# Cumulative log decays as rows through DRAM, in place of 32 products on TensorE

## The chip, the cores and the metric

The program runs on one core of a Trainium2 chip. The metric is device time in microseconds (us), taken as the median of several executions; beside them one execution was recorded by the hardware profiler.

## What is computed

The program runs two blocks on a sequence of 256 tokens of width 1024, all in fp32. The change lies in the hybrid mixer of the first block, and there in its Mamba-2 part (SSD), which has 16 heads in 2 groups of 8 and chunks of 128 tokens. Cut to what matters:

```python
a = (dt * A).reshape(b, nc, chunk, G, E)            # log decays
acs = jnp.cumsum(a, axis=2)                         # their sums along a chunk
seg = acs[:, :, :, None] - acs[:, :, None, :]       # (t, s) differences, per head
Lm = jnp.exp(jnp.where(mask, seg, -jnp.inf))        # causal decays
CB = jnp.einsum('bctgn,bcsgn->bctsg', C, B)
y_diag = jnp.einsum('bctsg,bctsge,bcsgep->bctgep', CB, Lm, xd)
```

For each of 2 chunks and 16 heads a 128x128 matrix of differences `seg` is needed: the sum at token t, which varies along the free dimension of a tile, less the sum at token s, which is the partition.

## The kernel before

Tokens come as two tiles of 128. Every large product is made as three products of fp32r halves (`mm3`, lines 277 to 279): each operand is split into a high part on ScalarE (`split`, line 203) and a low part on VectorE (line 207). Weights arrive by DMA in units of 1 MB into a ring of 3 buffers (`raw`, issued on the SyncE queue at line 258), and are split in halves into rings of 4 buffers (`hi`, `lo`). So a weight's load waits until the unit three earlier has been split, and a split waits until the products on the half four earlier are done. All these waits stand in the engines' own queues, which run strictly in order.

The hybrid mixer weaves two generators. `products` makes projections that need little beside TensorE; `chain` makes the SSD and then the mLSTM, and says at its yields how many steps of `products` go in between. The stages of `chain` that matter here:

- the log decays `a` (line 622) and, by products with the triangular mask `tri`, their sums by column, `cs` (lines 624 to 627);
- B and C: two weight groups, each followed by a causal convolution (`conv`, lines 635 to 642: one copy on ScalarE, then three dependent steps on VectorE) and a Silu into `bc`;
- `inputs(g)`: the same convolution for the x of one head group. Four accumulators `t2` come out of it, each turned by two TensorE transposes (line 663) that stand in TensorE's queue between the products;
- `states(g)`: the Silu of x, the factors of dt, and the chunk's state;
- `decays(g)`: for each chunk and head, line 687 multiplies the head's column of `a`, broadcast to 128 columns, with `tri`. This gives the sums as a row, the same on every partition; line 690 subtracts the column `cs` on VectorE and caps it, line 695 takes the exponential on ScalarE, and line 696 multiplies by the products of C and B;
- `outputs(g)`: the products with `seg`, gating and a norm.

Outside stretches that are marked `manual_schedule`, the order on each engine is not that of the code: a scheduler, which works with estimates of how long everything takes, sets it at build time. The hybrid part lies outside such stretches until its last projection.

Of the kernel before, what the change touches and what calls it, by code (L numbers as in the profile page):

```python
# [12 lines left out]
AF = mybir.ActivationFunctionType  # L13
# [91 lines left out]
class Net:  # L105
# [43 lines left out]
    def dram(self, shape):  # L149
        self.n += 1  # L150
        return self.dp.tile(shape, F32, name=f"dram{self.n}")

    def load_const(self, name, cols, parts=128):
        t = self.const(cols, parts=parts)
        self.nc.sync.dma_start(t, self.ins[name])
        return t
# [405 lines left out]
class Hybrid:  # L562
    def hybrid(self, then):
        nc = self.nc
        ins = self.ins
        V, A, PE, G = nc.vector, nc.scalar, nc.tensor, nc.gpsimd
        mm = PE.matmul
# [4 lines left out]
        def products():  # L572
# [24 lines left out]
            for g in range(2):  # L597
# [3 lines left out]
                    A.activation(so[t, g], p, AF.Sigmoid)  # L601
                yield

        def chain():

            fill = iter(FILL)
# [13 lines left out]
            V.memset(coef[:, 16:], -1.0)  # L620
            a = self.small(40).rearrange("p (t c) -> p t c", t=2)
            V.tensor_tensor(a, sp, coef[:, None, :].to_broadcast([128, 2, 20]), OP.mult)
            pc = self.pt()
            mm(pc[:, :40], self.tri, a.rearrange("p t c -> p (t c)"), start=True, stop=True)
            mm(pc[:, 64:80], self.after, a[:, 0, :16], start=True, stop=True)
            cs = self.small(40).rearrange("p (t c) -> p t c", t=2)
            V.tensor_copy(cs.rearrange("p t c -> p (t c)"), pc[:, :40])
            ecs, de = self.small(16), self.small(16)
            A.activation(ecs, cs[:, 1, :16], AF.Exp)
            A.activation(de, pc[:, 64:80], AF.Exp)  # L630
            dt = sp

            cw = self.col("hy_cw").rearrange("p (j k) -> p j k", k=5)
# [15 lines left out]
                    acc = conv(j, ps[i][:, :256])  # L649
                    A.activation(bc[:, j], acc.rearrange("p (t c) -> p t c", t=2), AF.Silu)  # L650

            xs, xd, st, px, seg, yv = {}, {}, {}, {}, {}, {}
            e8 = lambda z: z.rearrange("p (e q) -> p e q", e=8)

            def inputs(g):
# [23 lines left out]
            def decays(g):  # L679

                for c in range(2):
                    seg[c] = self.g().rearrange("p (e t) -> p e t", e=8)
                    for hb in range(2):
                        pr = self.pt().rearrange("p (e t) -> p e t", e=4)
                        for e in range(4):
                            h = g * 8 + hb * 4 + e
                            mm(pr[:, e, :], a[:, c, h:h + 1].to_broadcast([128, 128]), self.tri, start=True, stop=True)  # L687
                        for e in range(4):
                            h = g * 8 + hb * 4 + e
                            V.scalar_tensor_tensor(seg[c][:, hb * 4 + e, :], pr[:, e, :], cs[:, c, h:h + 1], self.cap,  # L690
                                                   op0=OP.subtract, op1=OP.min)
                for c in range(2):
                    for hb in range(2):
                        half = seg[c][:, hb * 4:hb * 4 + 4]
                        A.activation(half, half, AF.Exp)
                        V.tensor_tensor(half, half, cb[:, c, g, None, :].to_broadcast([128, 4, 128]), OP.mult)

            def outputs(g):
                for c in range(2):
                    py = e8(self.pt())  # L700
                    for e in range(8):
                        mm(py[:, e, :], seg[c][:, e, :], xd[c, g][:, e, :], start=True, stop=True)
                    dx = e8(self.t2())
                    G.tensor_tensor(dx, xs[c, g], self.row("hy_d")[:, g * 8:g * 8 + 8, None].to_broadcast([128, 8, 64]), OP.mult)
                    V.tensor_tensor(dx, py, dx, OP.add)
                    if c:
                        po = self.pt()
                        mm(po, bc[:, 2 + g, 1, :], st[g], start=True, stop=True)
                        yo = e8(self.t2())
                        V.tensor_tensor(yo, e8(po), ecs[:, g * 8:g * 8 + 8, None].to_broadcast([128, 8, 64]), OP.mult)  # L710
                        V.tensor_tensor(dx, dx, yo, OP.add)
                    y = yv[c] = dx.rearrange("p e q -> p (e q)")
                    V.tensor_tensor(y, y, zs[c][:, g * 512:(g + 1) * 512], OP.mult)
                    ss = self.small(1)
                    A.activation(self.junk[:, :512], y, AF.Square, accum_out=ss)
                    r = self.rsqrt(ss, 1, 1.0 / 512)
                    V.tensor_scalar(y, y, r, None, op0=OP.mult)

            def turn(g):
                for c in range(2):  # L720
                    self.flip(yv[c], cat_y, g, c, self.col("hy_sn")[:, 4 * g:4 * g + 4])
# [17 lines left out]
            yield next(fill)  # L739
            inputs(1)  # L740
            outputs(0)
            yield next(fill)
            turn(0)
            states(1)
# [37 lines left out]
            for hb in range(2):  # L782
                pr = self.pt().rearrange("p (h c s) -> p h c s", h=2, c=2)
# [22 lines left out]
            for h in range(4):  # L806
                p = self.pt()
# [4 lines left out]
            for c in range(2):  # L812
                for h in range(4):
                    p = self.pt()
# [10 lines left out]
            for c in range(2):  # L825
# [8 lines left out]
                r = self.rsqrt(ss, 4, 1.0 / 256)  # L834
# [975 lines left out]
```

## Time and profile before

| | |
|---|---|
| median of 3 executions | 1719.06 us (1717.37 to 1719.6) |
| the profiled execution | 1717.73 us |
| its span, first to last instruction | 1715.9 us |
| TensorE (PE) busy | 1686.2 us, 98% of the span |
| VectorE (DVE) busy | 1130.9 us, 66% |
| ScalarE (ACT) busy | 896.4 us, 52% |
| GpSimd (POOL) busy | 299.4 us, 17% |
| share of TensorE in the chain of work that ended last | 82% |
| mean granted TensorE clock | 0.992 of full speed |

The hybrid part takes about 204 to 360 us of the span, and the stages above lie between 215 and 300 us. In the profile's rows a TensorE instruction's end is modelled, so two rows that follow each other overlap; the time that one takes of the engine is the distance from its start to the next start. The same is true, less strongly, of the other engines. An fp32 product appears as two records.

### The profile page before, as it was taken

The numbers are of one execution on the slowest core, as the hardware profiler recorded it, in microseconds if no ns is written. First come the engines' busy times: TensorE is split into PE (matmuls) and PEld (weight loads), VectorE is DVE, ScalarE is ACT, GpSimd is POOL, SyncE is SP. The second block draws the span as 40 slices with busy tenths as digits, with TensorE's granted clock in tenths as the row PEclk, the third lists the DMA queues.
The fourth block names the chain that finished last, engine by engine and source line by source line (L and its number), as shares of the span: only waits on it lengthen the run. The fifth ranks groups of instructions, "written<-read, shape, count | busy, mean of one in ns | idle before, by whom it ended". The sixth has DMA issues, their size and how long they took to land.

```text
span 1715.9 us, 27060 instructions
## 1 busy us (share of the span) xinstructions
PE 1686.2 (98%) x10518; PEld 1495.0 (87%) x10518; DVE 1130.9 (66%) x2203; ACT 896.4 (52%) x1329; POOL 299.4 (17%) x458
## 2 busy tenths in 40 slices
PE   9999999999999999999899999999999999999998
PEld 8998799788999899988689998888898878889886
DVE  7665588656665566647956664657775765778566
ACT  7443476464444354434465444567446446644643
POOL 3000021002000010000331000234532113364211
PEclk9999999999999999999899999999999999999999
DMA  7555453444555555554125556445443544554442
GB/s 274 197 176 205 150 193 127 147 152 159 194 193 188 176 193 191 182 205 161 68 99 180 189 189 212 167 153 168 142 151 143 184 165 175 149 163 158 146 148 96
DMA packets 63440, 287.65 MB, mean 168 GB/s; under 512 B 23760, under 2 KB 26704, under 8 KB 30288
## 3 DMA queue, kind: packets, MB, share of 16 engines
q1 hardware_dynamic: 63312, 285.92, 48.3%
q8 instruction: 83, 1.36, 0.3%
q14 instruction: 45, 0.37, 0.1%
HBM read 283.28 MB, written 2.62 MB: 167 GB/s over the span
## 4 chain that ended last, share of the span: by engine, by line
PE 82%; DVE 6%; POOL 5%; issue 3%; ACT 2%; DMA 2%; SPq 0%; POOLq 0%; ACTq 0%; DVEq 0%
PE mm L278 25%; PE mm L279 25%; PE mm L277 24%; DVE lo L207 2%; POOL g L1343 2%; POOL g L1341 2%; DMA g<-dram 1%; PE tr L435 1%; ACT hi L203 1%; DVE g L85 0%; DVE g L1010 0%; PE tr L1275 0%; PE tr L1583 0%; PE tr L687 0%; PE tr L1401 0%
## 5 line engine op out<-in xcount | busy, mean ns | idle before, releaser
L207 DVE TENSOR_TENSOR lo<-raw,hi 128x512 fp32r<-128x512 f32 (+1 forms) x1032 | 696.5, 718 | 433.4 <-ACT hi L203 432.2
L203 ACT ACTIVATE hi<-raw 128x1024 fp32r<-128x1024 f32 (+1 forms) x526 | 546.7, 1045 | 542.9 <-PE mm L279 239.6
L278 PE MATMUL mm<-g,hi 128*128 128x256 f32 x1760 | 496.7, 282 | 0.0
L277 PE MATMUL mm<-g,hi 128*128 128x256 f32 x1760 | 495.3, 282 | 0.8 <-ACT hi L203 0.8
L279 PE MATMUL mm<-g,lo 128*128 128x256 f32 x1760 | 495.8, 283 | 0.0
L277 PEld LDWEIGHTS mm<-g,hi 128*128 128x128 f32 x1760 | 333.2, 189 | 2.2 <-ACT hi L203 1.2
L278 PEld LDWEIGHTS mm<-g,hi 128*128 128x128 f32 x1760 | 333.1, 189 | 0.7
L279 PEld LDWEIGHTS mm<-g,lo 128*128 128x128 f32 x1760 | 332.4, 189 | 0.3 <-issue 0.2
L277 PE MATMUL mm<-hi,g 128*128 128x512 f32 (+1 forms) x784 | 313.2, 400 | 0.7 <-ACT g L203 0.7
L278 PE MATMUL mm<-lo,g 128*128 128x512 f32 (+1 forms) x784 | 311.5, 398 | 1.2 <-DVE lo L207 0.7
L279 PE MATMUL mm<-hi,g 128*128 128x512 f32 (+1 forms) x784 | 309.6, 396 | 1.0 <-DVE g L448 1.0
L279 PEld LDWEIGHTS mm<-hi,g 128*128 128x128 f32 x784 | 147.7, 189 | 35.9 <-DVE g L448 1.9
L278 PEld LDWEIGHTS mm<-lo,g 128*128 128x128 f32 x784 | 148.1, 189 | 35.1 <-DVE lo L207 5.0
L277 PEld LDWEIGHTS mm<-hi,g 128*128 128x128 f32 x784 | 148.0, 189 | 32.5 <-ACT g L203 1.2
L278 PE MATMUL mm<-lo,f 128*128 128x512 f32 x416 | 164.7, 396 | 0.2 <-POOL lo L207 0.2
L279 PE MATMUL mm<-hi,f 128*128 128x512 f32 x416 | 163.9, 396 | 0.0
L277 PE MATMUL mm<-hi,f 128*128 128x512 f32 x416 | 161.4, 398 | 0.0
L214 POOL TENSOR_SCALAR sm<-sm 128x1 f32<-128x1 f32 x18 | 7.8, 431 | 576.7 <-ACT c L70 576.0
L278 PEld LDWEIGHTS mm<-lo,f 128*128 128x128 f32 x416 | 78.1, 188 | 19.5 <-POOL lo L207 0.6
L279 PEld LDWEIGHTS mm<-hi,f 128*128 128x128 f32 x416 | 78.1, 188 | 18.6
L277 PEld LDWEIGHTS mm<-hi,f 128*128 128x128 f32 x416 | 78.1, 188 | 18.2
L90 POOL TENSOR_TENSOR g<-x,g 128x512 f32<-128x512 f32 x12 | 15.4, 1292 | 216.1 <-DVE x L499 170.2
(408 smaller groups left out, 1666.8 us busy)
## 6 DMA issues: line engine op xcount, KB each, us to landing
raw<-in_wgw_dram SPq DMA_DIRECT2D x80, 1024.0 KB, 4.9
raw<-in_wdn_dram SPq DMA_DIRECT2D x44, 1024.0 KB, 4.9
raw<-in_bx_dram SPq DMA_DIRECT2D x24, 1024.0 KB, 4.8
raw<-in_bgate_dram SPq DMA_DIRECT2D x24, 1024.0 KB, 4.8
raw<-in_bw_dram SPq DMA_DIRECT2D x20, 1024.0 KB, 4.8
raw<-in_hyx_dram SPq DMA_DIRECT2D x12, 1024.0 KB, 4.8
raw<-in_bproj_dram SPq DMA_DIRECT2D x12, 1024.0 KB, 4.9
raw<-in_hyw_dram SPq DMA_DIRECT2D x10, 1024.0 KB, 4.9
```

What stands on the lines that cost most here:

```text
L90: self.nc.gpsimd.tensor_tensor(self.src[t][:, s], self.net.x[t][:, s], self.gain[:, s], OP.mult)
L203: nc.scalar.activation(hi, src, AF.Copy)
L207: (nc.gpsimd if o and help else nc.vector).tensor_tensor(lo[..., s], src[..., s], hi[..., s].bitcast(F32), OP.subtract)
L214: G.tensor_scalar(r, v, add, EPS, op0=OP.add, op1=OP.add)
L277: mm(out, a[0], b[0], start=start, stop=False)
L278: mm(out, a[0], b[1], start=False, stop=False)
L279: mm(out, a[1], b[0], start=False, stop=stop)
L435: self.nc.tensor.transpose(p[:, k, :], src[:, k * 128:(k + 1) * 128], self.ident)
L1341: G.tensor_tensor(a, Z[:, :m, e:e + 1].to_broadcast([128, m, n]), B[:, e:e + 1, cs].to_broadcast([128, m, n]), OP.mult)
L1343: G.tensor_tensor(Z[:, :m, cs], Z[:, :m, cs], a, OP.add)
```

## The change

The 32 products of line 687 go. Instead `rows` makes, for each chunk, one product of the 16 columns of `a` with `tri`: 16 rows (heads) of 128 sums. It copies both to SBUF, and writes them to DRAM, 16 KB. `spread` reads a run of 8 heads (4 KB) back with a partition step of zero, so that each of the 128 partitions gets the same 4 KB: one transfer of 512 KB into the `seg` tile for each chunk and head group, four in all. Line 690's subtraction (line 711 now) then works in place on that tile, one instruction for each head as before. In the code `rows` stands behind the convolutions of B and C, the first two spreads behind that, and the other two behind `outputs(0)`. The two new products, and the first subtraction of each `decays`, are held in program order.

```diff
+    def rows(self, products):
+
+        nc, n, b = self.nc, products[0][0].shape[-1], len(products)
+        p, r = self.pt(), self.t2()
+        for i, (cols, mask) in enumerate(products):
+            self.tc.keep_in_program_order(nc.tensor.matmul(p[:n, i * 128:(i + 1) * 128], cols, mask, start=True, stop=True))
+        nc.scalar.activation(r[:n, :b * 128], p[:n, :b * 128], AF.Copy)
+        d = self.dram([b, n, 128])
+        nc.sync.dma_start(d.rearrange("b n c -> n b c"), r[:n, :b * 128].rearrange("n (b c) -> n b c", b=b))
+        return d
+
+    def spread(self, out, d, first, n):
+
+        self.nc.sync.dma_start(out, bass.AP(d.tensor, d.offset + first * 128, [[0, 128], [1, n * 128]]))
...
+        def spread_seg(c, g, rows):
+
+            seg[c] = self.g().rearrange("p (e t) -> p e t", e=8)
+            self.spread(seg[c].rearrange("p e t -> p (e t)"), rows, c * 16 + g * 8, 8)
...
+            cs_rows = self.rows([(a[:, c, :16], self.tri) for c in range(2)])
             pc = self.pt()
             mm(pc[:, :40], self.tri, a.rearrange("p t c -> p (t c)"), start=True, stop=True)
...
+            for c in range(2):
+                spread_seg(c, 0, cs_rows)
...
                 for c in range(2):
-                    seg[c] = self.g().rearrange("p (e t) -> p e t", e=8)
-                    for hb in range(2):
-                        pr = self.pt().rearrange("p (e t) -> p e t", e=4)
-                        for e in range(4):
-                            h = g * 8 + hb * 4 + e
-                            mm(pr[:, e, :], a[:, c, h:h + 1].to_broadcast([128, 128]), self.tri, start=True, stop=True)
-                        for e in range(4):
-                            h = g * 8 + hb * 4 + e
-                            V.scalar_tensor_tensor(seg[c][:, hb * 4 + e, :], pr[:, e, :], cs[:, c, h:h + 1], self.cap,
+                    for e in range(8):
+                        h = g * 8 + e
+                        i = V.scalar_tensor_tensor(seg[c][:, e, :], seg[c][:, e, :], cs[:, c, h:h + 1], self.cap,
                                                    op0=OP.subtract, op1=OP.min)
+                        if c + e == 0:
+                            self.tc.keep_in_program_order(i)
...
             outputs(0)
+            for c in range(2):
+                spread_seg(c, 1, cs_rows)
             yield next(fill)
```

The code of `conv`, B and C moves up unchanged, ahead of the sums by column. The scheduler answers with another order on the engines. Line numbers of the changed kernel are higher: 654 is the convolution step of line 640, 222 the low part of line 207, 218 the high part of line 203, 690 the transposes of line 663, 719 the product of line 696, 718 the exponential of line 695, 651 the convolution's copy of line 637.

VectorE, from the sums by column on, in `inputs(0)`; before, `t2_333` and `t2_334` are accumulators of `inputs(0)`, `lo364` is the low part of a weight half:

```order
L627 COPY sm_301_2376<-tr_300_2373 128x40
L207 TENSOR_TENSOR lo358_2798<-raw357_2795,hi358_2797 128x512 x2
L640 SCALAR_TENSOR_TENSOR t2_333_2671<-mm_328_2609,c21_112,t2_333_2671 128x255
L640 SCALAR_TENSOR_TENSOR t2_333_2671<-mm_328_2609,c21_112,t2_333_2671 128x254
L207 TENSOR_TENSOR lo359_2803<-raw357_2795,hi359_2802 128x512 x2
L640 SCALAR_TENSOR_TENSOR t2_333_2671<-mm_328_2609,c21_112,t2_333_2671 128x253
L640 SCALAR_TENSOR_TENSOR t2_334_2678<-mm_329_2610,c21_112,t2_334_2678 128x255
L640 SCALAR_TENSOR_TENSOR t2_334_2678<-mm_329_2610,c21_112,t2_334_2678 128x254
L640 SCALAR_TENSOR_TENSOR t2_334_2678<-mm_329_2610,c21_112,t2_334_2678 128x253
L207 TENSOR_TENSOR lo364_2839<-raw363_2836,hi364_2838 128x512 x2
```

The same place now; `t2_331`, `t2_332`, `t2_338` and `t2_339` are the four accumulators, `g_322` and `g_323` the two tiles of the first spreads, `lo358` is the `lo359` of before:

```order
L654 SCALAR_TENSOR_TENSOR t2_332_2613<-mm_327_2545,c21_112,t2_332_2613 128x254
L654 SCALAR_TENSOR_TENSOR t2_338_2682<-mm_333_2620,c21_112,t2_338_2682 128x255
L654 SCALAR_TENSOR_TENSOR t2_331_2606<-mm_326_2544,c21_112,t2_331_2606 128x253
L654 SCALAR_TENSOR_TENSOR t2_332_2613<-mm_327_2545,c21_112,t2_332_2613 128x253
L654 SCALAR_TENSOR_TENSOR t2_338_2682<-mm_333_2620,c21_112,t2_338_2682 128x254
L222 TENSOR_TENSOR lo358_2792<-raw356_2784,hi358_2791 128x512 x2
L654 SCALAR_TENSOR_TENSOR t2_339_2689<-mm_334_2621,c21_112,t2_339_2689 128x255
L654 SCALAR_TENSOR_TENSOR t2_338_2682<-mm_333_2620,c21_112,t2_338_2682 128x253
L711 SCALAR_TENSOR_TENSOR g_322_2538<-g_322_2538,sm_319_2532,c7_80 128x128 x7
L654 SCALAR_TENSOR_TENSOR t2_339_2689<-mm_334_2621,c21_112,t2_339_2689 128x254
L711 SCALAR_TENSOR_TENSOR g_323_2540<-g_323_2540,sm_319_2532,c7_80 128x128 x8
L654 SCALAR_TENSOR_TENSOR t2_339_2689<-mm_334_2621,c21_112,t2_339_2689 128x253
```

Here the steps of four accumulators alternate, and 15 of the 16 subtractions of `decays(0)` stand ahead of the next weight half (`lo363`, two rows further on); before, they stood behind `states(0)`.

VectorE in `inputs(1)`, before, behind the low part of weight half 379; `t2_373` is the accumulator that TensorE turns first:

```order
L207 TENSOR_TENSOR lo395_3100<-raw394_3097,hi395_3099 128x512 x2
L640 SCALAR_TENSOR_TENSOR t2_373_2962<-mm_368_2900,c21_112,t2_373_2962 128x255
L640 SCALAR_TENSOR_TENSOR t2_373_2962<-mm_368_2900,c21_112,t2_373_2962 128x254
L207 TENSOR_TENSOR lo396_3105<-raw394_3097,hi396_3104 128x512 x2
L640 SCALAR_TENSOR_TENSOR t2_373_2962<-mm_368_2900,c21_112,t2_373_2962 128x253
```

The same place now; `g_391` and `g_392` are the tiles of the other two spreads, `t2_372` is the accumulator that is turned first, and its third step comes behind all of these:

```order
L222 TENSOR_TENSOR lo378_2975<-raw376_2967,hi378_2974 128x512 x2
L711 SCALAR_TENSOR_TENSOR g_391_3084<-g_391_3084,sm_319_2532,c7_80 128x128 x7
L222 TENSOR_TENSOR lo396_3093<-raw395_3090,hi396_3092 128x512 x2
L711 SCALAR_TENSOR_TENSOR g_392_3086<-g_392_3086,sm_319_2532,c7_80 128x128 x8
L719 TENSOR_TENSOR g_391_3084<-g_391_3084,l2_341_2701 128x512
L654 SCALAR_TENSOR_TENSOR t2_372_2951<-mm_367_2889,c21_112,t2_372_2951 128x255
L222 TENSOR_TENSOR lo397_3098<-raw395_3090,hi397_3097 128x512 x2
L654 SCALAR_TENSOR_TENSOR t2_373_2958<-mm_368_2890,c21_112,t2_373_2958 128x255
L719 TENSOR_TENSOR g_392_3086<-g_392_3086,l2_341_2701 128x512
L222 TENSOR_TENSOR lo402_3158<-raw401_3155,hi402_3157 128x512 x2
L654 SCALAR_TENSOR_TENSOR t2_372_2951<-mm_367_2889,c21_112,t2_372_2951 128x254
```

Of `decays(1)`, 15 of 16 subtractions and three of four products have moved from behind `outputs(0)` to the middle of the convolutions of `inputs(1)`, where the first of them waits for a transfer.

The SyncE queue, now, from the last weight unit ahead of the first spreads; without the five rows of lines 161 and 166 it is the order of before:

```order
L273 DMA raw369_2891<-in_hyw_dram 128x2048
L161 DMA dram317_2527<-t2_316_2523 16x2x128
L166 DMA g_322_2538<-dram317_2527 128x1024
L166 DMA g_323_2540<-dram317_2527 128x1024
L273 DMA raw376_2967<-in_hyw_dram 128x2048
L273 DMA raw395_3090<-in_hyw_dram 128x2048
L273 DMA raw401_3155<-in_hyw_dram 128x2048
L166 DMA g_391_3084<-dram317_2527 128x1024
L166 DMA g_392_3086<-dram317_2527 128x1024
L273 DMA raw415_3283<-in_hyw_dram 128x2048
```

Each spread stands right behind the load of a weight unit, and that load waits for a weight half's split on VectorE.

## Rows read from the trace of the kernel before

**Rows 1.** The page: busy time, share of the span and instructions of each engine.

```profile
PE 1686.2 (98%) x10518; PEld 1495.0 (87%) x10518; DVE 1130.9 (66%) x2203; ACT 896.4 (52%) x1329; POOL 299.4 (17%) x458
```

**Rows 2.** TensorE's waits, 200 to 345 us: who for whom, us, times, longest.

```profile
PE mm L278 <- DVE lo L207: 0.2, 1, 0.2
```

**Rows 3.** TensorE's timeline and line 687: start us, us, instruction; counts of records.

```profile
252.97 2.84 PE L687 MATMUL tr<-c,sm 128*128 128x128 f32 x24
255.56 0.36 PE L277 MATMUL mm<-g,hi 128*128 128x256 f32 x1
...
L687 PE MATMUL tr<-c,sm x64: 270/275/275, 253.0 to 297.1; 128*128 128x128 f32 x64
```

**Rows 4.** TensorE's timeline at the sums, at the first turns, and in inputs(1).

```profile
235.14 0.31 PE L624 MATMUL tr<-sm,c 128*128 128x40 f32 x2
...
237.40 0.83 PE L729 MATMUL tr<-g 128*128 128x128 f32 x6
...
271.83 0.38 PE L663 MATMUL tr<-c,t 128*128 128x128 f32 x2
```

**Rows 5.** ScalarE's timeline, 235 to 238 us: start us, us, instruction.

```profile
235.94 1.28 ACT L629 ACT_TABLE_LOAD   x1
...
237.71 0.56 ACT L637 ACTIVATE t<-mm,c 128x256 f32<-128x256 f32 x1
```

**Rows 6.** VectorE's timeline, 231 to 258 us: start us, us, instruction, idle before.

```profile
231.41 2.04 DVE L640 SCALAR_TENSOR_TENSOR t<-mm,c,t 128x255 f32<-128x255 f32 x5 [0.54 <-ACT t L637]
233.36 1.29 DVE L207 TENSOR_TENSOR lo<-raw,hi 128x512 fp32r<-128x512 f32 x2
...
247.59 2.14 DVE L670 TENSOR_TENSOR l<-l,sm 128x512 f32<-128x512 f32 x2 [0.62 <-ACT l L669]
249.66 1.53 DVE L673 TENSOR_TENSOR t<-l,sm 128x512 f32<-128x512 f32 x1
...
254.06 3.19 DVE L690 SCALAR_TENSOR_TENSOR g<-tr,sm,c 128x128 f32<-128x128 f32 x12 [0.47 <-PE tr L687]
257.17 0.68 DVE L696 TENSOR_TENSOR g<-g,l 128x512 f32<-128x512 f32 x1
```

**Rows 7.** DMA issues by tile: count, KB each, median us from issue to landing.

```profile
raw<-in_hyw_dram SPq DMA_DIRECT2D x10, 1024.0 KB, 4.9
g<-in_gains_dram SPq DMA_DIRECT2D x7, 512.0 KB, 5.7
g<-dram SPq DMA_DIRECT2D x12, 128.0 KB, 4.9
g<-in_fgain_dram SPq DMA_DIRECT2D x1, 512.0 KB, 3.2
c<-in_pos_dram SPq DMA_DIRECT2D x1, 1.0 KB, 6.2
```

**Rows 8.** SyncE's timeline at 138 us, at a transfer of the gains.

```profile
137.96 0.33 SPq L258 DMA_DIRECT2D raw<-in_wdn_dram  x1
138.34 0.43 SPq L59 DMA_DIRECT2D g<-in_gains_dram  x1
```

**Rows 9.** Lines 85 (from SBUF) and 499 (from PSUM): min/median/max ns.

```profile
L85 DVE SCALAR_TENSOR_TENSOR g<-x,sm,g x16: 742/746/753, 194.2 to 1406.9; 128x512 f32<-128x512 f32 x16
...
L499 DVE SCALAR_TENSOR_TENSOR x<-mm,sm,x x16: 741/748/751, 190.1 to 1093.1; 128x512 f32<-128x512 f32 x16
```

**Rows 10.** TensorE: waits; then stretches with PE, PEld, DVE, ACT, POOL, PEclk, DMA.

```profile
PE tr L1252 <- ACT t L1248: 3.0, 2, 1.5
...
1124.05:1127.46 3.41, 3.41 (x17) 3.41 (x18) 1.29 (x2) 1.18 (x2) 2.73 (x9) 0.50 0.16 34
1127.46:1130.88 3.42, 3.42 (x18) 3.42 (x18) 1.29 (x2) 0.38 (x1) 1.97 (x6) 0.51 0.69 273
1434.68:1438.09 3.41, 3.41 (x19) 3.41 (x18) 2.05 (x4) 1.06 (x1) 2.81 (x8) 0.51 0.45 118
```

More of the change, by code (lines that the diff above doesn't have):

```diff
@@ L602, in products @@
                 yield
+        seg = {}
+        def spread_seg(c, g, rows):
+            seg[c] = self.g().rearrange("p (e t) -> p e t", e=8)
+            self.spread(seg[c].rearrange("p e t -> p (e t)"), rows, c * 16 + g * 8, 8)
         def chain():
@@ L622, in chain @@
             V.tensor_tensor(a, sp, coef[:, None, :].to_broadcast([128, 2, 20]), OP.mult)
[L623 to L630, printed above, removed]
             dt = sp
@@ L650, in chain @@
                     A.activation(bc[:, j], acc.rearrange("p (t c) -> p t c", t=2), AF.Silu)
-            xs, xd, st, px, seg, yv = {}, {}, {}, {}, {}, {}
+            cs_rows = self.rows([(a[:, c, :16], self.tri) for c in range(2)])
+            pc = self.pt()
+            mm(pc[:, :40], self.tri, a.rearrange("p t c -> p (t c)"), start=True, stop=True)
+            mm(pc[:, 64:80], self.after, a[:, 0, :16], start=True, stop=True)
+            cs = self.small(40).rearrange("p (t c) -> p t c", t=2)
+            V.tensor_copy(cs.rearrange("p t c -> p (t c)"), pc[:, :40])
+            ecs, de = self.small(16), self.small(16)
+            A.activation(ecs, cs[:, 1, :16], AF.Exp)
+            A.activation(de, pc[:, 64:80], AF.Exp)
+            for c in range(2):
+                spread_seg(c, 0, cs_rows)
+            xs, xd, st, px, yv = {}, {}, {}, {}, {}
             e8 = lambda z: z.rearrange("p (e q) -> p e q", e=8)
```

## The prediction, made before the changed kernel ran

> **What bounds the kernel now.** The page comes first: TensorE is busy for 1686.2 of 1715.9 us, VectorE for 66% [rows 1]. So what TensorE doesn't have to do is time saved, unless it waits for something new. The next view is TensorE's waits in the hybrid part: between 200 and 345 us the one wait for a weight split lasts 0.2 us, and none is for a convolution [rows 2]. TensorE runs without a gap there, and VectorE has idle time that nobody waits for. Last come the timelines of TensorE, ScalarE and VectorE [rows 3 to 6], to put the changed order on the clock of this trace, and the landings of transfers [rows 7, 8].
>
> **What is removed.** 24 records of line 687 take from 252.97 to 255.56, 108 ns each, and there are 64 [rows 3]: 6.9 us, all of it on TensorE's path, half in each `decays`. Added on TensorE are two products, four records, 0.4 us. By this account alone the kernel gains 6.5 us. VectorE keeps its 32 subtractions; 12 of them took from 254.06 to 257.17, 0.26 us each [rows 6], with PSUM as the source.
>
> Does SBUF as a source make them quicker? A 512-column instruction of the same kind takes 746 ns from SBUF and 748 from PSUM [rows 9], so I take 0.26 us for the new ones too. The Trainium skill, "VectorE: DVE Perf Modes", section "The TRN2 errata", gives 58 cycles of fixed cost from SBUF against 120 from PSUM at 0.96 GHz, an estimate of 65 ns saved on each; with some 31 of them ahead of the second stall below, the stall would end up to 2.0 us earlier and the sum would be 1721.7. The rows show no such difference, so it isn't counted.
>
> **What is moved: first stall.** TensorE's queue holds the transposes of the convolved x between products, in order. In `inputs(0)` the first to be turned is `t2_331`. ScalarE now has, behind the high part that ends where its table load stands at 235.94 [rows 5], the copy of the new rows: their products stand at 235.14 on TensorE [rows 4], so the copy starts at once, some 0.35 us. Then come two convolution copies (0.45 each), the table load (1.28), two small exponentials (0.2) and the copy for `t2_338` (0.55) [rows 5]: 239.2. VectorE runs the first step of `t2_338` (0.4; five steps took 1.95 us [rows 6]) ahead of the third of `t2_331` (0.5): 240.1. TensorE is there when its products are through, 237.40 [rows 4] plus 0.4: it waits some 2 us, where it waited for nothing before.
>
> **The transfers.** The write of the rows stands behind the load of unit 369, which goes out when the split before it is done, at about 235, and lands 4.9 us later [rows 7]. 1 KB that was issued behind loads took 6.2 us [rows 7], so I let the 16 KB land no sooner than that load: 240. A 512 KB transfer with nothing before it lands in 3.2 us, one issued 0.4 us behind a 1 MB load in 5.7 [rows 7, 8]. These move 128 rows of 4 KB from DRAM as the spreads do, but from different addresses; no row shows 128 reads of the same 4 KB. The bounds are 3.2 and 5.7 from below (I see no reason for less), and from above four times what a 128 KB read in small pieces takes, 4.9 us [rows 7], so 20 us. I take the lower ones, since size and rows are theirs. First spread: 243.2.
>
> **Second stall.** From 240.1 VectorE has four steps and one split (two instructions, 1.2 us [rows 6]): 242.9, so it barely waits for the first spread. From 243.2 it has 15 subtractions (3.9), two steps (0.8), three products of line 719 (0.6 each), three splits (3.6): 253.3. Then `states(0)`, 1.0 + 1.5 us [rows 6] and some 0.5 for ScalarE, one subtraction and a split: 258. That split sets off the load of unit 401 and, right behind it, the third spread at 258.4: landing 5.7 later, 264.0. VectorE has 4 us of work until 262 and waits 2. Behind that wait stand the split of half 396 and all steps of `inputs(1)`, and on ScalarE the copy for `t2_372` stands behind the exponential of the same tile. From 264.0: 15 subtractions 3.9, three products 1.8, four splits 4.8, six steps 2.4, and the third step of `t2_372` 0.5: 277.4. Before, TensorE passed its first transposes of `inputs(1)` at 271.83 [rows 4] without waiting. So it is 5.6 us late here. The first stall and the first half of the saving are inside that figure, since TensorE now waits for VectorE and not for its own past. Still to come is the second half of the saving, 3.45 us, as 16 of the 32 products of before stand behind this place. Net: 2.2 us later.
>
> Do the weights hold? The 15 subtractions delay the split of half 363 to 249.7, and TensorE asks for it at about 251. The cover is the four buffers of split halves; a first spread 2 us later would use it up.
>
> **The clock.** Two stalls of 2 and about 7 us may cost more than themselves. Line 1252 made TensorE wait 1.5 us twice [rows 10]; thereafter the granted clock stood at 0.5, that is 1.2 GHz, for 6.8 us once (two rows) and for 3.4 us once (the third), with TensorE busy throughout. At half speed this loses 3.4 and 1.7 us. For the second stall I take 2.4, near the middle; what the first costs is inside the second, whose end VectorE sets.
>
> **Sum.** 2.2 + 2.4 = 4.6 us. The profiled execution took 1717.73 us, 1.8 more than its span; that gives 1722.3 for it, and the same step on the median, which lies 1.3 above it, 1723.7 us.
>
> **Rivals.**
> TensorE alone decides: the scheduler's order holds, no stall, 6.5 us gained, 1712.6. For it: no wait in this part before, 34% of VectorE idle. Against: the third step of `t2_372` stands behind 15 subtractions that can't start before a transfer lands.
> The two cancel: the second stall is some 3 us shorter, because the third spread lands 2 us sooner than the gains did and the copies on ScalarE slip past, and the clock doesn't fall: 1717. For it: VectorE's wait at that place is only 2 us of the stall. Against: it takes both.
> Slow spreads: 128 partitions read the same 4 KB of DRAM, and a transfer takes twice as long. The first lands 3.2 us later, the third another 5.7, and both reach the second stall: 2.2 + 8.9, with the clock 13.5 us, so 1732. It decides from the point where the first spread lands later than VectorE's 242.9, and pays nearly in full from there. For it: pieces of DRAM read in other patterns were far slower for their size [rows 7]. Against: size and row length are those of the gains.
> That the products stay is excluded by the order: no product of line 687 is left on TensorE.
>
> **How the numbers follow.** Forecast (stalls as above, 1719.5 to 1728): 0.62, about a quarter of it below 1722.5. Slow spreads, 1728 to 1740: 0.16. Cancelled, 1715.6 to 1719.5: 0.14. TensorE alone: 0.08. A measurement of this kernel tells about 0.2%, 3.4 us, from no change. So faster, below 1715.6: 0.08; same, up to 1722.5: 0.14 + 0.16 = 0.30; slower: 0.62. The range from 1716 to 1732 leaves out the gain and about half of the slow spreads.
>
> **What would show it.** In the changed trace: no record of line 687's product, and some 6.5 us less busy time for it; waits of TensorE's transposes (line 690) for VectorE, about 2 us near 238 and 7 near 271 to 278; a wait of VectorE (line 711) for a transfer near 262; landings of the spreads between 3 and 6 us; a clock of 0.5 for 3 to 7 us behind the second stall. If line 690 waits for nothing, the second stall is wrong and the gain stands. If the spreads take over 8 us, the slow rival holds. If the wait is at a weight split (lines 292 to 294 for `lo363`), the cover was thinner than I put it.

## The result, and the profile of the changed kernel

The changed kernel takes 1730.4 us (median of 20 executions) against 1718.2 us before (20); the ratio over all executions, rather than of the medians, is 1.0089, 95% interval 1.0066 to 1.0113. So it is slower, 12 us at the medians, where 5 were forecast. In most kernels here some executions lie up to 20 us above the rest at a lower mean clock; so below each kernel is told by its median and by a stretch of its profile that these later clock drops don't touch.

That stretch runs from the first to the second group of line 85 on VectorE, the norms at the entry of the hybrid part and of the part behind its feed-forward. Source view of line 85, of the kernel before: ns min/median/max, first and last start in us, form.

```profile
L85 DVE SCALAR_TENSOR_TENSOR g<-x,sm,g x4: 742/746/752, 194.2 to 203.6; 128x512 f32<-128x512 f32 x4
...
L85 DVE SCALAR_TENSOR_TENSOR g<-x,sm,g x4: 744/746/752, 784.2 to 793.6; 128x512 f32<-128x512 f32 x4
```

The same of the changed kernel:

```profile
L85 DVE SCALAR_TENSOR_TENSOR g<-x,sm,g x4: 743/744/751, 197.0 to 206.4; 128x512 f32<-128x512 f32 x4
...
L85 DVE SCALAR_TENSOR_TENSOR g<-x,sm,g x2: 747/750/752, 797.2 to 797.9; 128x512 f32<-128x512 f32 x2
```

Before, the stretch is 784.2 - 194.2 = 590.0 us; now 600.2, 10.2 more. The profiled execution took 1737.3 us, 19.6 more than that of before. The rest is not the change's stretch: 2.8 us were lost ahead of it (197.0 against 194.2; the profiles of the experiments begin it between 194.2 and 196.2), and 6.6 behind it, in the sparse attention, by a lower clock (last section). Times of the changed kernel below are 2.8 us late against those of before for that reason.

The page, in answer to [rows 1]:

```profile
PE 1693.5 (98%) x10458; PEld 1500.1 (86%) x10458; DVE 1130.6 (65%) x2203; ACT 895.8 (52%) x1330; POOL 298.6 (17%) x458
```

60 records of TensorE fewer (64 gone, 4 new), and yet its busy time rose by 7 us: it worked slower. Its waits, 200 to 345 us, in answer to [rows 2] (who for whom, us, times, longest):

```profile
PE tr L690 <- DVE t L654: 9.2, 1, 9.2
PE tr L690 <- ACT hi L218: 1.8, 1, 1.8
PE tr L450 <- DVE g L85: 0.5, 1, 0.5
```

Two new waits, both at the transposes of line 690, the two that were forecast. TensorE's timeline at both, in answer to [rows 4]:

```profile
237.68 0.61 PE L158 MATMUL tr<-c,sm 128*16 128x128 f32 x4
238.22 0.41 PE L669 MATMUL tr<-sm,c 128*128 128x40 f32 x2
...
242.70 0.41 PE L690 MATMUL tr<-c,t 128*128 128x128 f32 x2 [1.77 <-ACT hi L218]
...
283.15 0.66 PE L690 MATMUL tr<-c,t 128*128 128x128 f32 x2 [9.18 <-DVE t L654]
```

The first wait is put down to a high part that had long been done; what came last is the third step of `t2_331` on VectorE. Its timeline, in answer to [rows 6]:

```profile
239.49 1.64 DVE L654 SCALAR_TENSOR_TENSOR t<-mm,c,t 128x255 f32<-128x255 f32 x4
241.69 1.65 DVE L654 SCALAR_TENSOR_TENSOR t<-mm,c,t 128x255 f32<-128x255 f32 x4 [0.55 <-ACT t L651]
...
247.22 1.93 DVE L711 SCALAR_TENSOR_TENSOR g<-g,sm,c 128x128 f32<-128x128 f32 x7 [1.90 <-DMA g<-dram]
...
269.62 1.93 DVE L711 SCALAR_TENSOR_TENSOR g<-g,sm,c 128x128 f32<-128x128 f32 x7 [4.26 <-DMA g<-dram]
...
275.38 0.47 DVE L654 SCALAR_TENSOR_TENSOR t<-mm,c,t 128x255 f32<-128x255 f32 x1
...
282.14 2.80 DVE L654 SCALAR_TENSOR_TENSOR t<-mm,c,t 128x255 f32<-128x255 f32 x7
```

At 241.69 a step of `t2_338` waits for ScalarE's copy, and the third step of `t2_331` stands behind it. At 247.22 and 269.62 the subtractions wait for a spread, 1.9 and 4.3 us. The three steps of `t2_372` begin at 275.38; the third is the second of the seven at 282.14, and at 283.15 TensorE turns it. SyncE's timeline, and the landings of the write and the four spreads, in answer to [rows 7, 8]:

```profile
238.72 0.33 SPq L161 DMA_DIRECT2D dram<-t  x1
242.92 0.82 SPq L166 DMA_DIRECT2D g<-dram  x2
...
262.19 0.90 SPq L166 DMA_DIRECT2D g<-dram  x2
265.42 0.33 SPq L273 DMA_DIRECT2D raw<-in_hyw_dram  x1
...
dram<-t SPq DMA_DIRECT2D x1, 16.0 KB, 4.1
...
DMA to landing us min/median/max: 4.3/6.6/8.2
```

The fastest is the first (242.92 to 247.22), the third takes 7.4 us (262.19 to 269.62). The load of the next weight unit (415) goes out 3.2 us behind it, at 265.42, when VectorE has done the splits that stand ahead of its wait. The last view is the stretches around the second stall, in answer to [rows 10] (stretch, us, busy PE, PEld, DVE, ACT, POOL, granted clock, DMA share, GB/s):

```profile
274.00:277.00 3.00, 0.00 (x0) 0.00 (x0) 3.00 (x9) 3.00 (x6) 0.00 (x0) 1.00 0.00 0
277.00:283.00 6.00, 0.00 (x0) 0.00 (x0) 6.00 (x14) 0.90 (x2) 0.00 (x0) 0.51 0.53 175
283.00:294.00 11.00, 10.85 (x46) 9.85 (x47) 5.99 (x11) 4.38 (x6) 3.37 (x4) 0.50 0.28 97
294.00:297.00 3.00, 3.00 (x27) 3.00 (x26) 3.00 (x6) 0.25 (x1) 0.11 (x1) 0.97 0.00 0
```

Within the stall, at about 277, the clock falls to 0.50, 1.2 GHz, and stays there to 294: 17 us, 11 of them with TensorE busy. At full speed that work would have taken half as long, so some 5.5 us are lost (an estimate).

### The profile page after: what moved, and what is told of

It reads as the page before. It is cut to its first block, busy times and chain, and to the rows that moved or that the text cites. A ratio compares the mean times of both kernels' runs of the same rounds, so it can differ in the third digit from the quotient of the medians.

```text
span 1735.5 us, 26955 instructions
## 1 busy us (share of the span) xinstructions
PE 1693.5 (98%) x10458; PEld 1500.1 (86%) x10458; DVE 1130.6 (65%) x2203; ACT 895.8 (52%) x1330; POOL 298.6 (17%) x458
## 4 chain that ended last, share of the span: by engine, by line
PE 82%; DVE 5%; POOL 4%; ACT 3%; issue 3%; DMA 2%; SPq 0%; POOLq 0%; ACTq 0%; DVEq 0%
PE mm L293 25%; PE mm L294 24%; PE mm L292 24%; POOL g L1368 2%; DVE lo L222 2%; POOL g L1366 2%; DMA g<-dram 1%; PE tr L450 1%; ACT hi L218 1%; PE tr L725 1%; DVE g L85 0%; DVE g L1035 0%; PE tr L1300 0%; PE tr L1426 0%; PE tr L1608 0%
```

## The experiments

The theory: the products' time is gained in full; a first stall comes from the rows on ScalarE and the order of the steps; a second from the subtractions ahead of the convolution steps, lengthened by the spreads; and the clock that falls in it costs as much again. The rivals: the products' time was hidden anyway, the transfers themselves cost the time, or the clock falls for a reason of its own. Diffs are against the changed kernel, or the kernel before where that is said. "Stretch" is that of line 85, less 590.0 us.

### The products taken out, no transfers

```diff
-                            mm(pr[:, e, :], a[:, c, h:h + 1].to_broadcast([128, 128]), self.tri, start=True, stop=True)
...
-                            V.scalar_tensor_tensor(seg[c][:, hb * 4 + e, :], pr[:, e, :], cs[:, c, h:h + 1], self.cap,
+                            i = V.scalar_tensor_tensor(seg[c][:, hb * 4 + e, :], self.tri, cs[:, c, h:h + 1], self.cap,
...
+                            self.tc.keep_in_program_order(i)
```

> The kernel before without its 32 products: the subtraction reads the constant triangular mask in place of the products' rows, so the differences are wrong and that part of the computation is left out. No rows, no transfers; the subtractions are held behind the x of their own head group, so that they stand where they stood. My theory (the products lay on TensorE's path, and their time is all that they cost): 6.9 us less TensorE time, no new wait, 1711 to 1712 against 1718. Rival (they filled time in which TensorE would have waited for VectorE or a weight anyway): 1716 to 1718, with the time back as waits of TensorE between 250 and 300 us.

Against the kernel before. 1712.8 us against 1718.9, stretch -5.9, no new wait of TensorE. The interval of the ratio, 0.9953 to 1.0016, does not exclude no change, but eight of the ten executions (1710.2 to 1715.2) lie below all 33 of the kernel before (from 1715.9). The gain is real, 6 us of the 6.9.

### The transfers alone

```diff
+            cs_rows = self.rows([(a[:, c, :16], self.tri) for c in range(2)])
+            for c in range(2):
+                self.spread(self.g(), cs_rows, c * 16, 8)
...
             outputs(0)
+            for c in range(2):
+                self.spread(self.g(), cs_rows, c * 16 + 8, 8)
```

> The kernel before with the rows, their write and four spreads added at the places of the changed kernel, into tiles that nobody reads; the 32 products stay. My theory (the transfers themselves cost nothing, the rows' copy on ScalarE and the order around it cost the first stall): two small products 0.4 us, a stall of TensorE of 0 to 2 us near 240, no second stall, clock at full speed: 1718 to 1721. Rival (the spreads push weight loads back, TensorE waits for splits): 1723 or more, with waits of lines 277 to 279 for a split, and the clock down behind them.

Against the kernel before. 1723.1 us, stretch +5.2: over the theory's range and within the rival's, but not for the rival's reason: no split is waited for. (In this kernel line 681 is the transposes of line 690, and 655 the convolution step.) TensorE's waits, and the stretch behind the first:

```profile
PE tr L681 <- DVE t L655: 2.2, 1, 2.2
...
241.00:245.00 4.00, 4.00 (x17) 3.43 (x16) 2.89 (x7) 0.87 (x2) 0.00 (x0) 0.57 0.93 255
```

The first stall is there without any subtraction having moved, 2.2 us, and this one takes the clock along (0.57 over 4 us; 3.4 us at half speed). The stall, some 1.7 us for the clock and 0.5 for the new products make 4.4 of the 5.2 us. TensorE waits for nothing else that is new.

### The subtractions held in program order

```diff
-                        if c + e == 0:
+                        if True:
                             self.tc.keep_in_program_order(i)
```

> The changed kernel with one edit: all 32 subtractions are held in program order, not only the first of each group, so that those of the second group stand behind the convolutions of inputs(1) again and those of the first behind states(0). Products out, transfers in. My theory (the loss is the place of the subtractions ahead of the convolution steps, and the clock that falls in the stall): the wait of 9.2 us goes, no half speed near 280, the first wait of 1.8 us may stay; 1718.2 less 6.5 plus 0 to 2, so 1712 to 1714. Rival (the slow transfers cost it wherever the subtractions stand, since a product then waits for the differences): 1722 or more, with TensorE waiting for the products of the decays.

1715.3 us, stretch -3.3; against the kernel before 0.999, interval 0.9974 to 1.0007. TensorE's waits and the stretch where the second stall was:

```profile
PE tr L690 <- ACT hi L218: 1.8, 1, 1.8
...
270.00:290.00 20.00, 20.00 (x169) 19.52 (x168) 18.74 (x39) 12.63 (x19) 4.83 (x6) 1.00 0.40 139
```

One edit, and of the 12 us nothing is left: no second stall, full clock. All four transfers are still made. But the third goes out some 9 us sooner and takes 5.9 us, so this run alone doesn't part the transfers from the place of the subtractions; the run with one group held, below, does. With the subtractions behind them, the three steps of `t2_372` also stand nearly together again.

### The second stall filled with work

```diff
+FILLER = 42
...
+                        for n in range(FILLER if g and gr + i == 0 else 0):
+                            self.tc.keep_in_program_order(mm(px[g][1][:, 384:], self.ident, self.tri, start=True, stop=True))
                         for t in range(2):
                             PE.transpose(px[g][t][:, (2 * gr + i) * 128:(2 * gr + i + 1) * 128],
```

> The changed kernel with 42 products of two constants (two records of 108 ns each, 9.0 us) put into TensorE's queue right ahead of the first transposes of inputs(1), into a buffer that these overwrite: TensorE works where it waited 9.2 us. My theory (TensorE's idling lets the clock fall; 17 us at half speed lose some 6.5 us): the clock stays at full speed there and the time falls by 5 to 7 us, to 1723 to 1725, though TensorE does no more useful work. Rival A (the clock falls by itself or for another engine's sake): half speed stays, 1730 or more. Rival B (the clock costs nothing net, since TensorE waits for VectorE afterwards anyway): clock up, time unchanged within 2 us.

1725.4 us, 5.0 less than the changed kernel; stretch +8.2, 2.0 less. The stretches from the filler on:

```profile
268.00:278.00 10.00, 8.74 (x78) 8.54 (x77) 10.00 (x27) 3.63 (x6) 0.00 (x0) 1.00 0.39 134
278.00:290.00 12.00, 11.76 (x100) 11.72 (x101) 7.43 (x15) 3.75 (x6) 0.19 (x1) 1.00 0.34 127
```

TensorE works in place of waiting, and the clock stays up: so it falls for TensorE's idling. Useless work made the kernel faster. The stretch shows 2.0 us of it: the filler and a wait of 1.5 us behind it took 1.6 us more than the stall did, and 3.4 us at half speed came later, between 341 and 346 (some 1.7 us), which leaves 2.2 of the 5.5. Why the medians gain 5.0 isn't shown. Nor is the filler all that differs: the scheduler gave `inputs(1)` another order, with one split in place of three between the first and the third step of `t2_372`.

### The spreads on another queue

```diff
-        self.nc.sync.dma_start(out, bass.AP(d.tensor, d.offset + first * 128, [[0, 128], [1, n * 128]]))
+        self.nc.gpsimd.dma_start(out, bass.AP(d.tensor, d.offset + first * 128, [[0, 128], [1, n * 128]]))
```

> The changed kernel with one edit: the four spreads are issued by GpSimd instead of SyncE, so that the third and the fourth no longer stand behind the load of unit 401 and go out with the first two; VectorE's order in the stretch stays nearly that of the changed kernel. My theory (of the second stall's 9.2 us, VectorE's wait for the third spread, 4.3 us, is a part, the subtractions ahead of the convolution steps are the rest): no wait of VectorE for a transfer near 265, a stall of 4 to 6 us near 270, some half speed still, 1723 to 1727. Rival A (the transfer decides all of it): no stall, 1715. Rival B (the place decides all of it, the transfer is hidden): stall of 9 us, 1730.

The four executions took 1726.6, 1729.2, 1748.3 and 1748.7 us, so no gain is shown by them; stretch +9.0, 1.2 less than the changed kernel. Line 702 is the product of the chunk's state in `states(0)`. VectorE's subtractions of the second group, then TensorE's waits:

```profile
266.93 1.92 DVE L711 SCALAR_TENSOR_TENSOR g<-g,sm,c 128x128 f32<-128x128 f32 x7
...
PE tr L690 <- DVE t L654: 5.3, 2, 4.9
PE tr L702 <- DVE t L700: 2.1, 1, 2.1
```

Nothing waits for the third spread any more, and a stall of 4.9 us remains: the place of the work on VectorE makes a stall without that wait. The 4.3 us by which it is shorter are not the transfer's share, though VectorE's wait was as long. With four spreads issued at once the second lands after 8.4 us; VectorE waits 2.7 and 2.4 us for the first group's and begins the second group only 1.0 us sooner than in the changed kernel, counted from line 85. TensorE passes the transposes 1.4 us sooner and gets there 2.9 us later, mostly for the waits of 2.1 us and 0.4 us ahead of it. So what the wait for the third spread costs by itself isn't shown. Half speed still lasted 13.7 us.

### Other rows as the source

```diff
-            self.spread(seg[c].rearrange("p e t -> p (e t)"), rows, c * 16 + g * 8, 8)
+            nc.sync.dma_start(seg[c].rearrange("p e t -> p (e t)"), ins["gains"][1])
```

> The changed kernel with the spreads reading 512 KB of a gains input, 128 different rows of 4 KB, in place of the same 4 KB 128 times; the sums are not used, so the differences are wrong. The first two need not wait for the write of the rows. My theory (a spread is slow because it shares the engines with the loads around it, not because of its source): the third lands 6 to 9 us after its issue as before. Rival (reading the same 4 KB from 128 partitions costs extra): it lands in 3 to 6 us and VectorE's wait of 4.3 us shrinks by 2 us or more.

One execution, 1730.6 us. The third transfer lands after 5.8 us, in the rival's range, and VectorE's wait falls from 4.3 to 1.1 us. But the third spread, the same 4 KB for all, landed after 5.6 to 5.9 us in six other runs on the same queue, and after 6.9 to 7.4 in four. So the source does not decide it. What goes along with it is the next weight load: in the four slow cases it went out 3.2 us behind the third spread (as at 265.42 in the changed kernel), in the six others 8 us or more behind it, when the spread had landed. No run changes that alone, so it is a finding and not a shown cause. In this run the scheduler put the first subtractions, which no longer wait, between the steps of `inputs(0)`, and the first stall grew to 6.1 us; the second was 5.3: stretch +11.8.

### One group held, and steps held as well

Three runs held other things: the subtractions of the second group alone (`if g or c + e == 0`); all of them and every convolution step (e5_both_held); all of them and the steps of `inputs(0)`. The expectations call the run with all subtractions held, above, e3_order_held, and the products taken out e1_products_out.

> The changed kernel with the subtractions of the second group alone held in program order; those of the first still stand 15 of 16 ahead of the split of half 363. My theory (the four buffers of split halves cover the first group's place; only the second group's place costs): as e3_order_held, 1714 to 1716, with the first wait of 1.8 us and no other. Rival (the first group's place delays the later splits and so shares in the loss): 1718 or more, with TensorE waiting for a split or a convolution between 250 and 290.

1717.9 us, stretch -3.4, as with all held; the only wait over 0.5 us is the first stall's 1.8. The landing of the third spread, issued at 260.15; VectorE's first steps of `inputs(1)` and its subtractions of the second group; TensorE's wait:

```profile
g<-dram SPq DMA_DIRECT2D x1, 512.0 KB, 7.1
...
266.73 1.00 DVE L654 SCALAR_TENSOR_TENSOR t<-mm,c,t 128x255 f32<-128x255 f32 x2 [0.79 <-ACT t L651]
...
286.49 3.76 DVE L711 SCALAR_TENSOR_TENSOR g<-g,sm,c 128x128 f32<-128x128 f32 x14
...
PE tr L690 <- ACT hi L218: 1.8, 1, 1.8
```

This is the cleanest of the runs. Counted from line 85 the third spread goes out within 0.3 us of where it does in the changed kernel, and it is nearly as slow, 7.1 us against 7.4; yet nothing waits for it, and the second stall is gone. So the stall needs the second group's subtractions ahead of the convolution steps; a slow spread alone doesn't make it. The first group's place made no wait: no split came too late, as the theory said of the four buffers. The median is over the range, though the profile isn't.

> e3_order_held with one more edit: the convolution steps on VectorE are held in program order too, so the three steps of an accumulator stand in one piece again and the first one to be turned in inputs(0) no longer waits behind a step of a later one. My theory (the first stall, 1.8 us, comes from these interleaved steps behind ScalarE's copy of the rows and its table load): the wait goes, 1715.3 less 1.8 is 1713 to 1714, near e1_products_out. Rival (the rows' copy itself delays ScalarE and TensorE arrives early anyway): the wait stays at 1 to 2 us, 1715 to 1716.

1717.2 us, stretch -3.2: a miss. The first stall fell to 0.2 us (at 240.4), but a wait of 0.6 for a split (261.4) and one of 0.4 at the transposes of `inputs(1)` (272.9) came up, and no time was won.

> e3_order_held with the convolution steps of inputs(0) alone held in program order as well; those of B, C and inputs(1) stay free. In e5_both_held, where all were held, the first stall fell to 0.4 us, but a wait of 0.6 us for a split came up and the time was no better than that of e3_order_held. My theory (each of the two stalls goes with the order that makes it, and what is left of the change is the products' time less 0.5 us for the new ones): no wait of TensorE over 0.6 us in the hybrid part, 1712.5 to 1714.5. Rival (holding steps moves the wait to another place, as in e5_both_held): 1715 to 1717, with waits of 1 us or more in all.

1718.5 us, stretch +0.5: a miss, the rival holds, and by more than it said. The first stall is 0.2 us here too; the 0.4 us that the expectation takes from the run before for it stood in `inputs(1)`. New are 0.6 us for a split (261.0) and 1.2 us at the transposes of `inputs(1)` (273.2), with 6.8 us at half speed behind it.

### The changed kernel again

> The changed kernel as it is, profiled once more. Its first profile has, beside the 17 us at half speed behind the second stall, one stretch of 10 us more at half speed near 845 us, in the sparse attention, than the kernel before. My theory (that stretch comes and goes by execution and is no part of the change): this profile has the stall of about 9 us and 14 to 17 us at half speed near 280 again, one stretch at half speed near 850, and a time of 1727 to 1732. Rival (the shift of the later work by the change brings it about): the additional stretch is there again, 1736 to 1738.

1747.8 us, stretch +9.8, a stall of 8.4 us, 17 us at half speed. So the hybrid part repeats. Behind 840 the clock fell again, for longer than the first time. The sparse attention, where the code is that of before, cost the first profile 6.5 us more than the kernel before, and this one 20.5 (from the second to the third group of line 85). Neither side had it right: the drop differs by execution, but it was there both times. Why, is open.

### The rows made later

```diff
             inputs(0)
+            cs_rows = self.rows([(a[:, c, :16], self.tri) for c in range(2)])
+            for c in range(2):
+                spread_seg(c, 0, cs_rows)
```

with the subtractions held, and the same lines gone from their former place; the second run holds the steps of `inputs(1)` too.

> All 32 subtractions held as in e3_order_held, and the rows, their write and the first two spreads moved in the code behind inputs(0): ScalarE's copy of the rows now comes behind the convolution copies of inputs(0), and VectorE's order up to the first turns is that of the kernel before. The steps of inputs(1) alternate between accumulators as in the changed kernel, but without subtractions ahead of them. My theory (the first stall comes with the rows' place in front of the first turns, and the subtractions of the first group, at about 256, have time for a spread that starts 6 us later): no stall near 240, at most 1 to 2 us in inputs(1): 1712 to 1715. Rival (the spread now lands too late for the first group): TensorE waits for the products of decays(0) or for a split behind it, 1717 or more.

> e11_rows_later with the convolution steps of inputs(1) held in program order too. My theory: the alternating steps of inputs(1) are worth at most 1 to 2 us, so 1712 to 1714, the same as e11_rows_later or up to 2 us less. Rival (as in e5_both_held and e9_first_turns_held, holding steps brings waits at other places): 1716 or more.

1735.1 and 1726.4 us, stretches +5.4 and +4.0: both missed. The first median says little, as no execution lies between 1728.8 and 1741.5; the profiled ones took 1723.2 and 1723.9 us. The first stall is gone, as expected, and what the first rival named, a wait for the products of the decays or for a split behind them, did not come. But TensorE's timeline of the first run has (line 687 is the transposes here, 708 the subtractions)

```profile
276.12 0.66 PE L687 MATMUL tr<-c,t 128*128 128x128 f32 x2 [5.52 <-DVE t L654]
```

and VectorE's shows why:

```profile
259.33 4.28 DVE L708 SCALAR_TENSOR_TENSOR g<-g,sm,c 128x128 f32<-128x128 f32 x16
...
269.55 0.48 DVE L654 SCALAR_TENSOR_TENSOR t<-mm,c,t 128x255 f32<-128x255 f32 x1
...
272.74 1.26 DVE L654 SCALAR_TENSOR_TENSOR t<-mm,c,t 128x254 f32<-128x254 f32 x3
...
275.11 2.81 DVE L654 SCALAR_TENSOR_TENSOR t<-mm,c,t 128x255 f32<-128x255 f32 x7
```

No subtraction stands ahead of the steps of `inputs(1)` but the first group's, as in the kernel before. They alternate between accumulators with splits between, so that `t2_372`'s three take from 269.55 to about 275.9, and TensorE waits 5.5 us. In the run with order held they took 2.6 us, from 268.60 to 271.2. So these end 4.7 us later: 1.0 is the later start, the rest what stands between them, steps and splits, which can make a second stall without a subtraction among them. Holding the steps of `inputs(1)` didn't keep splits out from between them, nor a first step of another accumulator (4.3 us of wait).

No run that computes the same is shown to beat the kernel before. Holding the subtractions beats the changed kernel, and the products taken out show what was to be had, some 6 us.

## Why the prediction was wrong

The sign, both stalls and their places were right; the size was not. The steps that failed are two terms of the sum, the landing of the spreads in the second stall (2.9 us short) and the clock behind it (3.1 us short). By its steps, against the changed kernel's profile less the 2.8 us of late start:

**The products.** 6.9 us forecast, 0.4 for the new ones; measured 5.9 to 6.1 in the run without them, and 0.54 (237.68 to 238.22).

**The subtractions from SBUF.** I put them at 0.26 us as from PSUM. Sixteen in a row take 4.2 us in the run with order held, from the first start (255.84) to the next instruction's (260.04), 0.26 each. The figures of the Trainium skill, "VectorE: DVE Perf Modes", section "The TRN2 errata", by which each would save 65 ns, are not borne out here.

**The first stall.** 2 us forecast, 1.8 measured, with the mechanism named: the copy of the rows, then the table load, then the copy for `t2_338`. ScalarE's timeline:

```profile
238.33 0.37 ACT L159 ACTIVATE t<-tr 16x256 f32<-16x256 f32 x1 [0.18 <-PE tr L158]
238.61 0.99 ACT L651 ACTIVATE t<-mm,c 128x256 f32<-128x256 f32 x2
239.62 1.28 ACT L674 ACT_TABLE_LOAD   x1
...
241.09 0.56 ACT L651 ACTIVATE t<-mm,c 128x256 f32<-128x256 f32 x1
```

**The transfers** were mis-sized. The first spread was put at 3.2 us, the lower bound, and took 4.3; VectorE waited 1.9 us, where I had it barely wait, and so the third went out 1.0 us later than forecast (259.4 against 258.4). The third was put at 5.7 and took 7.4, with the load of the next weight unit 3.2 us behind it, which the prediction didn't see coming; where none came so soon, 5.6 to 5.9 us were measured. It landed at 266.8, not 264.0. From there to the third step of `t2_372` I counted 13.4 us, and it is 13.4 (269.62 to about 283.0). The write landed as put, 0.2 us behind the load ahead of it (240.1).

**The second stall** is right in kind: 5.6 us late forecast; the transposes now come at 283.15 against 271.83, less 2.8: 8.5. The difference, 2.9, is the transfers', 2.8 by the third's landing. Net of the saving still to come 5.1 us, not 2.2. What I had not seen as a cause of its own, though the sum held it, is the alternation of the steps, with the splits between them.

**The clock** was the other mis-sized term. I took 2.4 us from stretches of 3.4 and 6.8 us at half speed behind stalls of 1.5 us, though the stall was to be 7 us long. It was 11 busy us at half speed, 5.5 us lost. 5.1 + 5.5 = 10.6, against 10.2 in the stretch. The trace of the kernel before has a nearer row, which the prediction leaves out: in the sparse attention TensorE waits 5.2 us for GpSimd, until 833.7, and the clock stands at half speed from 830 to 844. The wait, then the stretches (columns as above):

```profile
PE tr L1062 <- POOL t L926: 5.2, 1, 5.2
...
830.50:833.92 3.42, 0.23 (x1) 0.24 (x2) 3.28 (x12) 1.07 (x2) 1.60 (x3) 0.50 0.00 0
833.91:837.33 3.42, 3.42 (x13) 2.55 (x12) 3.25 (x10) 1.88 (x2) 3.25 (x5) 0.50 0.00 0
837.33:840.74 3.41, 2.88 (x7) 2.15 (x7) 3.34 (x6) 0.00 (x0) 1.80 (x2) 0.50 0.10 19
840.74:844.15 3.41, 3.41 (x11) 2.42 (x10) 3.27 (x13) 0.00 (x0) 1.86 (x2) 0.51 0.91 326
```

TensorE is busy for 9.9 us of it, so some 5 us are lost. With 5 in place of 2.4 the sum is 7.2 us, not 4.6.

**What remains.** The medians differ by 12.2 us, the stretch by 10.2; where the other 2 us lie isn't shown.

**The rivals.** The time lies in the band of the slow spreads (1728 to 1740), and the spreads were slower than forecast. But that rival was to double them, and they bring 2.9 of the missing us, the clock 3.1; that the time lies in its band does not bear it out. TensorE alone (1712.6) comes nearer with one line more: in the run with order held the transfers stay, the second stall goes, the first stays, and the time is 1715.3.

**The covers** held: no wait for a split of `lo363`, as said, though VectorE reached the subtractions 1.2 us later than put. That TensorE ran without a gap before overlooks 0.5 us of wait at line 435, near 204 us, which both kernels have (line 450 above).

## What to carry to other kernels

When work leaves the bounding engine and its replacement waits for a transfer, look at what now stands behind the waiting instruction in its queue: here 15 subtractions and the alternating steps that TensorE waited for, worth over twice the gain with the clock that fell; holding the subtractions in program order took that away. Price the clock behind a stall of TensorE by rows with a stall nearly as long: 9.2 us cost 5.5 more here, and a wait of 5.2 us in the trace of before had shown 5. For a transfer look also at what is issued behind it: the third spread took 7.4 us here with a load 3.2 us behind it, and 5.6 to 5.9 in the runs without one so near.

## What was not expected of the hardware

Stalls and what the granted clock did behind them, from the profiles: 1.8 us, none at half speed in the two runs that had this one alone; 2.2 us, 3.4 us at half speed; 4.3 us, 10.2; 4.9 and 5.5 us, 13.7; 8.4 and 9.2 us, 17.1. But waits of 1.2 and 0.6 us were followed by 6.8, and in the run with other rows 6.1 us by 6.8 and 5.3 us by 10.2, so the longest stall alone doesn't set it. In the two long ones the clock fell while TensorE stood idle and came back only after 11 to 12 us of work. The write of 16 KB took 4.1 us when it was issued 0.9 us behind a load, and 2.5 when it was issued 2.6 us behind one: in every profile with the write it landed 0.2 us behind that load. In the profiles of the changed kernel the clock fell again in the sparse attention, 560 us later; stretches of both kernels there, first before, then the changed one:

```profile
860.00:870.00 10.00, 10.00 (x71) 8.49 (x69) 5.32 (x31) 8.28 (x30) 2.71 (x6) 1.00 0.01 2
870.00:880.00 10.00, 10.00 (x57) 8.25 (x57) 6.00 (x15) 6.90 (x18) 3.04 (x2) 1.00 0.24 83
```

```profile
860.00:870.00 10.00, 8.14 (x34) 6.27 (x33) 7.22 (x30) 6.05 (x21) 1.41 (x2) 0.71 0.01 2
870.00:880.00 10.00, 10.00 (x51) 8.86 (x49) 4.68 (x20) 5.90 (x15) 4.15 (x6) 0.61 0.00 0
```

Before, TensorE is back at full speed by 845; here it falls once more behind 864, for 13.7 us. In the two profiles of about 1748 us, the changed kernel again and the spreads on another queue, this second drop lasts 44 us; no profile of the other experiments has one.
